# Probability buffers, the place of the late products and the bank of the second retention half in a two-layer decoder trunk

## The chip, the cores and the metric

The kernel runs on one core of one Trainium2 chip. The metric is the device time of one execution in microseconds, the median of several runs. TensorE multiplies matrices; ScalarE, VectorE and GpSimd work on elements; SyncE issues the transfers. In the rows these are PE (products) and PEld (weight loads), ACT, DVE, POOL and SP.

## The reference

Two layers, each on a residual stream of 256 tokens by 1024 channels. What matters here is the mixer, cut to its core:

```python
h = rmsnorm(x, norm_mix[i]); z = h @ w_in[i]           # q, k, v, gates, retention, merge columns
# attention, 2 groups of 4 heads, 2 blocks of 128 queries: three branches
p_cmp = masked_softmax(q @ k_cmp.T * scale, ...)       # 16 compressed keys
p_slc = masked_softmax(q @ k_s.T * scale, causal)      # all blocks are selected at this length
p_win = masked_softmax(q @ k_w.T * scale, causal)      # the window holds all 256 keys
y = g0 * (p_cmp @ v_cmp) + g1 * (p_slc @ v_s) + g2 * (p_win @ v_w)
# retention, 4 heads, chunks of 128
r = rms_noaffine((q_r @ k_r.T * decay) @ v_r) * silu(gate)
mix = sigmoid(merge_a) * (y @ w_up_nsa) + sigmoid(merge_b) * (r @ w_up_ret)
x = x + mix @ w_out
x = x + square(relu(rmsnorm(x) @ w_ff1)) @ w_ff2
x = x + sigmoid(rmsnorm(x) @ w_ple_gate) * (p @ w_ple)
```

## The kernel before

Everything is float32, and each matrix product with weights is three products of halves. A weight unit (128 x 1024) is loaded to a raw tile by SyncE and split into a high part (ScalarE copy, `hi`) and a low part (VectorE subtraction, `lo`), several units ahead of its use. A unit of 24 products of 256 columns is the usual grain. The units come in a fixed plan: first the columns of `w_in` (`kcvc`, `kvg`, `q`, `ksvs`, the compression weights `w`, retention `rq`, `rk`, `rv`, `rg`), then the merge columns `ma` and `mb` (8 units each), the up-projections `ua` and `ub` (4 each), `out`, and the MLP and the gated embedding.

The order on TensorE is that of the program text; the other engines' instructions are put in order by a scheduler from their dependences and priorities. While the kernel is built, a small planner keeps a virtual time for TensorE and for each other engine (`vt`, `charge`) and decides where the attention's and the retention's steps stand between the products of the weight units. These steps are generators in a background list. `poke`, called after each group of six products (three in the units of 512 columns), runs each generator whose due time is past; a generator yields its next due time, and `SLACK` adds to it by its name (1.0 for `attend`). The generators `attend` and `collect` also wait while ScalarE or VectorE is booked over 7 us ahead.

`attend` runs `softmax(g, t)` for the four turns (group, query block) and then the retention's `scores`. `softmax` issues per head the score products into two score banks of PSUM (`s_tile`), the masked maximum on VectorE and the exponentials on ScalarE into a probability tile `e`, and at the end the factor `cf` (gate over row sum). Its score products are due at the planned end of the bank's last reader (`sfin`) less `DE`. There are two probability buffers: one slot for the first query block (`S4` or `S2`), `S7` for the second, so the third and fourth softmax wait until the first and second turn are weighed. `collect` runs `weigh(g, t)` in the same order: GpSimd multiplies each block of `e` by its factor (3 blocks for the first query block, 5 for the second), TensorE transposes the block (`turn`), ScalarE and VectorE make high and low parts (`pp`, or `PC` for the 16 compressed keys), and two products add it to the accumulator bank `ot` (`apply`), of which there is one (`o_tile`). At the end `ot` is evacuated (`o`, two ScalarE and two VectorE instructions) and split to `NHh` and `NHl`, the input of `ua`. After the last turn `collect` runs `retain`: per query block the products of scores and values into `ot`, ScalarE's scaled copy, a norm with GpSimd's power, the gate, a transpose and a split, the input of `ub`.

The merge tensors `T` (tanh of `ma`, `mb`) lie in `S5` and `S6`; `S6` held `qn` before, `S7` held `ZB` before the probabilities and holds `MH` after them.

Of the kernel before, what the change touches and what calls it, by code (L numbers as in the profile page):

```python
# [15 lines left out]
P = 128  # L16
# [78 lines left out]
def trunk(ctx: ExitStack, tc: tile.TileContext, xT, wu, wg, cst, msk, par, pin, out):  # L95
# [34 lines left out]
    def o_tile(shape):  # L130
        return ps.tile(shape, F32, tag="ot", name=nm("ot"), bufs=1)
# [7 lines left out]
    def big(shape, tag, name, dt=F32):  # L139
        return bp.tile(shape, dt, tag=tag, name=nm(name))  # L140
# [39 lines left out]
    def fresh(t=None):  # L180
        cur[0] = vt["pe"] if t is None else t
# [191 lines left out]
    SL = 0.0  # L373
    DE = 0.5
    AHEAD_OF_SPLITS = ("compress",)
# [145 lines left out]
    def layer(l, st):  # L521
# [12 lines left out]
        qT = big([P, NH, S], "S3" if st["slot"] == 1 else "S1", "qT", F32R)  # L534
        e_tags = ["S4" if st["slot"] == 1 else "S2", "S7"]
        nc.gpsimd.memset(zs, 0.0)
# [120 lines left out]
        es, weighed, sfin, freed = {}, set(), [0.0, 0.0], [0.0]  # L657

        def softmax(g, t):
            e = big([P, HG, 272 if t == 0 else 528], e_tags[t], "e")  # L660
            nmx = small([P, HG, 3], "nmx")
# [32 lines left out]
            tt(out=cf, in0=cf, in1=gates[:, t, g * HG:(g + 1) * HG, :], op=ALU.mult)  # L694
            es[g, t] = e, cf

        def weigh(g, t):
            e, cf = es.pop((g, t))
            if t == 0:
                blocks = [(0, P, 0, V[:, 0, 0, g, :]), (144, P, 2, V[:, 1, 0, g, :]),  # L700
                          (128, 16, 1, VC[:, g, :])]
            else:
                blocks = [(0, P, 0, V[:, 0, 1, g, :]), (128, P, 0, V[:, 0, 0, g, :]),
                          (272, P, 2, V[:, 1, 0, g, :]), (400, P, 2, V[:, 1, 1, g, :]),
                          (256, 16, 1, VC[:, g, :])]
            n = len(blocks) - 1
            ot = o_tile([P, HG, P])
            parts = {}

            def scale(i):  # L710
                o, w, b, _ = blocks[i]
                gp(out=e[:, :, o:o + w], in0=e[:, :, o:o + w],
                   in1=cf[:, :, b:b + 1].to_broadcast([P, HG, w]), op=ALU.mult)

# [19 lines left out]

            fin, scaled = [], []
            t0 = cur[0]
            for i in range(n + 1):
                fresh(t0)
                scale(i)
                scaled.append(cur[0] + 3.0)  # L740
            yield scaled[0]
            turn(0)
            fin.append(cur[0])
            for i in range(1, n + 1):
# [5 lines left out]
                apply(i - 1)  # L750
            yield fin[n]
            apply(n)
# [18 lines left out]
        def attend():  # L771
            yield from until(lambda: NEED <= done)
            yield vt["pe"] + 1.5
            for i, x in enumerate(turns):
                if i > 1:
                    yield from until(lambda: turns[i - 2] in weighed)
                yield from softmax(*x)
            yield from until(lambda: (1, 0) in weighed)
            yield from scores()
            done.add("s")  # L780
# [27 lines left out]
        def scores():  # L808
            while not {("r", i, t) for i in range(2) for t in range(2)} <= done:
                yield vt["pe"] + 0.3  # L810
            d = big([P, 2, RH, 2, P], e_tags[0], "rs")
            sc_[0] = d
# [12 lines left out]
        def retain():  # L825
# [7 lines left out]
            for t in range(2):  # L833
                yield freed[-1]
                py = o_tile([P, RH, P])
                for h in range(RH):
# [158 lines left out]
        while not NEED <= done:  # L995
            pe_wait(vt["pe"] + 0.5)
            poke()
        T = [big([P, 8, S], f"S{5 + i}", "T") for i in range(2)]
        for i, name in enumerate(("ma", "mb")):
            for j in range(4):  # L1000
                pm = mm_tile([P, 2, S])
# [39 lines left out]
        drain()  # L1041
        MH = big([P, 8, S], "S7", "MH", F32R)
        ML = big([P, 8, S], "S8", "ML", F32R)
# [277 lines left out]
```

## Time and profile before

| | |
|---|---|
| time, median of 3 runs | 858.99 us (858.91 to 859.61) |
| the profiled execution | 859.11 us, its span 857.3 us |
| TensorE busy in the span | 842.5 us, 98% |
| VectorE, ScalarE, GpSimd busy | 602.6, 500.1, 78.6 us |
| TensorE clock granted, mean | 0.999 of 2.4 GHz |
| the weight load queue (q1) | 151.04 MB, 56.0% of 16 engines |

The page gives for each engine its busy time, and then the span in 40 slices with the busy share in tenths. A timeline row is: start in us, duration, engine, line, operation, what is written and read with shapes, the count of merged instructions, and in brackets the engine's idle time ahead of it and what ended that. The line named is mostly that of a helper (L220 products, L225 transposes, L188 ScalarE, L192, L200 and L208 VectorE, L214 GpSimd), so groups are told apart by their tiles. A wait row gives engine, line, releaser: us in total, times, the longest.

### The profile page before, as it was taken

How to read it: one execution, taken by the hardware profiler on the slowest of the kernel's cores; microseconds unless marked ns; L12 is line 12 of the kernel's file. 1: busy time of each engine (PE TensorE's matmuls, PEld its weight loads, DVE VectorE, ACT ScalarE, POOL GpSimd, SP SyncE). 2: the span in 40 equal slices, each digit the busy share in tenths (PEclk: the TensorE clock that was granted, in tenths of full speed). 3: DMA queues.
4: the chain of work that ended last, by engine and by line, in shares of the span. 5: the costliest groups of instructions: out<-in, count | busy, mean ns of one | idle time of the engine just before them, and what ended most of it. 6: DMA issues, size and time to landing. Idle time of an engine off the chain costs nothing.

```text
span 857.3 us, 16518 instructions
## 1 busy us (share of the span) xinstructions
PE 842.5 (98%) x6647; PEld 816.4 (95%) x6647; DVE 602.6 (70%) x977; ACT 500.1 (58%) x836; POOL 78.6 (9%) x68
## 2 busy tenths in 40 slices
PE   8999999999999999999999999999999999999997
PEld 7888899999999999999999988999999999999997
DVE  6897787686955555557789978776877555555584
ACT  6786876544744444445567768655456444445461
POOL 1240232010000000000004004121000000000000
PEclk9999999999999999999999999999999999999999
DMA  8877444356556665656555653643556656665641
GB/s 265 308 243 237 124 148 124 123 160 182 184 178 190 180 193 178 193 178 220 198 193 166 214 190 84 187 125 112 180 165 200 194 177 193 177 192 180 189 125 50
DMA packets 44284, 152.11 MB, mean 177 GB/s; under 512 B 5168, under 2 KB 6960, under 8 KB 44208
## 3 DMA queue, kind: packets, MB, share of 16 engines
q1 hardware_dynamic: 44064, 151.04, 56.0%
q8 instruction: 52, 0.85, 0.4%
q14 instruction: 24, 0.20, 0.1%
q10 hardware_dynamic: 144, 0.01, 0.0%
HBM read 149.99 MB, written 1.05 MB: 176 GB/s over the span
## 4 chain that ended last, share of the span: by engine, by line
PE 86%; DVE 6%; ACT 4%; DMA 1%; issue 1%; POOL 1%; SPq 0%; DVEq 0%; ACTq 0%; POOLq 0%
PE mm L220 49%; PE sc L220 17%; PE pt L220 14%; PE ot L220 4%; PE pt L225 2%; DVE lo L192 2%; ACT e L188 1%; ACT hi L188 1%; DMA raw<-in_wu_dram 1%; DVE e L208 1%; POOL e L214 0%; DVE o L192 0%; DVE zt L192 0%; ACT tmp L188 0%; ACT T L188 0%
## 5 line engine op out<-in xcount | busy, mean ns | idle before, releaser
L192 DVE TENSOR_TENSOR lo<-raw,hi 128x1024 fp32r<-128x1024 f32 (+2 forms) x287 | 345.3, 1210 | 186.7 <-ACT hi L188 185.5
L188 ACT ACTIVATE hi<-raw 128x1024 fp32r<-128x1024 f32 (+2 forms) x287 | 296.0, 1038 | 267.8 <-PE mm L220 155.6
L220 PE MATMUL mm<-XH,hi 128*128 128x256 f32 x992 | 283.6, 286 | 0.0
L220 PE MATMUL mm<-XH,lo 128*128 128x256 f32 x992 | 279.7, 282 | 0.0
L220 PE MATMUL mm<-XL,hi 128*128 128x256 f32 x992 | 279.4, 282 | 0.0
L220 PEld LDWEIGHTS mm<-XH,hi 128*128 128x128 f32 x992 | 187.0, 189 | 1.8
L220 PEld LDWEIGHTS mm<-XL,hi 128*128 128x128 f32 x992 | 187.0, 188 | 1.6
L220 PEld LDWEIGHTS mm<-XH,lo 128*128 128x128 f32 x992 | 186.9, 188 | 0.0
L220 PE MATMUL sc<-ho,hi 128*128 128x256 f32 x512 | 96.8, 282 | 0.0
L220 PE MATMUL pt<-ho,hi 128*128 128x256 f32 x512 | 96.6, 281 | 0.0
L220 PEld LDWEIGHTS sc<-ho,hi 128*128 128x128 f32 x512 | 78.6, 188 | 0.0
L220 PEld LDWEIGHTS pt<-ho,hi 128*128 128x128 f32 x512 | 78.6, 188 | 0.0
L220 PE MATMUL sc<-ho,lo 128*128 128x256 f32 x256 | 72.0, 281 | 0.0
L220 PE MATMUL pt<-ho,lo 128*128 128x256 f32 x256 | 72.0, 281 | 0.0
L220 PEld LDWEIGHTS pt<-ho,lo 128*128 128x128 f32 x256 | 48.2, 188 | 0.0
L220 PEld LDWEIGHTS sc<-ho,lo 128*128 128x128 f32 x256 | 48.2, 188 | 0.0
L214 POOL TENSOR_TENSOR e<-e,acf 128x512 f32<-128x512 f32 (+1 forms) x32 | 37.4, 1198 | 110.2 <-ACT hi L188 40.0
L220 PE MATMUL mm<-hi,XH 128*128 128x512 f32 (+2 forms) x128 | 44.4, 347 | 0.0
L220 PE MATMUL mm<-lo,XH 128*128 128x512 f32 (+2 forms) x128 | 43.7, 342 | 0.4 <-DVE lo L192 0.4
L220 PE MATMUL mm<-hi,XL 128*128 128x512 f32 (+2 forms) x128 | 43.7, 341 | 0.0
L188 ACT ACTIVATE e<-e,nmx 128x128 f32<-128x128 f32 (+2 forms) x96 | 37.6, 394 | 5.5 <-DVE nmx L208 5.2
L214 POOL TENSOR_TENSOR rso<-rsv,mhalf 128x2 f32<-128x2 f32 (+3 forms) x18 | 28.5, 1588 | 126.2 <-DVE rsv L196 126.2
(190 smaller groups left out, 1342.4 us busy)
## 6 DMA issues: line engine op xcount, KB each, us to landing
raw<-in_wu_dram SPq DMA_DIRECT2D x275, 512.0 KB, 3.7
raw<-in_wg_dram SPq DMA_DIRECT2D x8, 280.0 KB, 3.9
cst<-in_cst_dram SPq DMA_DIRECT2D x1, 768.0 KB, 6.3
out_dram<-XT SPq DMA_DIRECT2D x3, 256.0 KB, 2.4
XT<-in_xT_dram SPq DMA_DIRECT2D x4, 128.0 KB, 2.8
raw<-in_wu_dram SPq DMA_DIRECT2D x4, 128.0 KB, 3.3
XT<-in_xT_dram SPq DMA_DIRECT2D x2, 256.0 KB, 6.0
tmp<-in_pin_dram SPq DMA_DIRECT2D x2, 256.0 KB, 3.8
```

The lines of the kernel that those rows point to most:

```text
L188: return nc.scalar.activation(o, *a, **k)
L192: return nc.vector.tensor_tensor(**k)
L208: return nc.vector.tensor_tensor_reduce(**k)
L214: return nc.gpsimd.tensor_tensor(**k)
L220: return nc.tensor.matmul(o, a, b_, **k)
L225: return nc.tensor.transpose(o, a, i)
```

## The change

- There are three probability buffers: the first and third softmax use the slot they had, the second `S7`, the fourth `S6`. Only the third softmax still waits (for the first weighing).
- The factor's multiplications are issued at the end of `softmax`, right behind `cf`, instead of at the start of `weigh`; the planner puts the first transposes of a block at the planned end of its multiplication plus 1.6 instead of 3.0. The block of 16 compressed keys moves from the last place into the middle.
- The last product of a weighing is due `LATE` = 0.9 after the planned end of its low part, instead of at it; `DE` goes from 0.5 to 0.4.
- The second half of the retention's products goes into a score bank instead of the accumulator bank and is no longer held back by its planned release; the first half waits for the score banks' last planned reader too.
- `T` of `mb` moves to `S7` and is allocated when `mb` begins, and `MH` moves to `S6`.

```diff
@@ -371,7 +371,8 @@
     bg = []
     LB = 7.0
     SL = 0.0
-    DE = 0.5
+    DE = 0.4
+    LATE = 0.9
     AHEAD_OF_SPLITS = ("compress",)
     SLACK = {"kv_tail": 4.0, "q_tail": 3.0, "compress": 0.3, "attend": 1.0, "collect": 0.0}
 
@@ -532,7 +533,8 @@
         zs = big([P, 2, 16, 32], "B4", "zs")
         ZB = big([P, 16, 2, 2, 32], "S7", "ZB", F32R)
         qT = big([P, NH, S], "S3" if st["slot"] == 1 else "S1", "qT", F32R)
-        e_tags = ["S4" if st["slot"] == 1 else "S2", "S7"]
+        spare = "S4" if st["slot"] == 1 else "S2"
+        e_tags = {(0, 0): spare, (0, 1): "S7", (1, 0): spare, (1, 1): "S6"}
         nc.gpsimd.memset(zs, 0.0)
 
 
@@ -656,8 +658,16 @@
 
         es, weighed, sfin, freed = {}, set(), [0.0, 0.0], [0.0]
 
+        def branches(g, t):
+
+            if t == 0:
+                return [(0, P, 0, V[:, 0, 0, g, :]), (128, 16, 1, VC[:, g, :]),
+                        (144, P, 2, V[:, 1, 0, g, :])]
+            return [(0, P, 0, V[:, 0, 1, g, :]), (128, P, 0, V[:, 0, 0, g, :]), (256, 16, 1, VC[:, g, :]),
+                    (272, P, 2, V[:, 1, 0, g, :]), (400, P, 2, V[:, 1, 1, g, :])]
+
         def softmax(g, t):
-            e = big([P, HG, 272 if t == 0 else 528], e_tags[t], "e")
+            e = big([P, HG, 272 if t == 0 else 528], e_tags[g, t], "e")
             nmx = small([P, HG, 3], "nmx")
             sm = small([P, HG, 3], "smx")
             for h in range(HG):
@@ -692,25 +702,22 @@
             ts(out=cf, in0=sm, scalar1=1e-30, scalar2=None, op0=ALU.max)
             nc.vector.reciprocal(out=cf, in_=cf)
             tt(out=cf, in0=cf, in1=gates[:, t, g * HG:(g + 1) * HG, :], op=ALU.mult)
-            es[g, t] = e, cf
+            blocks = branches(g, t)
+            scaled = []
+            t0 = cur[0]
+            for o, w, b, _ in blocks:
+                fresh(t0)
+                gp(out=e[:, :, o:o + w], in0=e[:, :, o:o + w],
+                   in1=cf[:, :, b:b + 1].to_broadcast([P, HG, w]), op=ALU.mult)
+                scaled.append(cur[0] + 1.6)
+            es[g, t] = e, blocks, scaled
 
         def weigh(g, t):
-            e, cf = es.pop((g, t))
-            if t == 0:
-                blocks = [(0, P, 0, V[:, 0, 0, g, :]), (144, P, 2, V[:, 1, 0, g, :]),
-                          (128, 16, 1, VC[:, g, :])]
-            else:
-                blocks = [(0, P, 0, V[:, 0, 1, g, :]), (128, P, 0, V[:, 0, 0, g, :]),
-                          (272, P, 2, V[:, 1, 0, g, :]), (400, P, 2, V[:, 1, 1, g, :]),
-                          (256, 16, 1, VC[:, g, :])]
+            e, blocks, scaled = es.pop((g, t))
+
             n = len(blocks) - 1
             ot = o_tile([P, HG, P])
             parts = {}
-
-            def scale(i):
-                o, w, b, _ = blocks[i]
-                gp(out=e[:, :, o:o + w], in0=e[:, :, o:o + w],
-                   in1=cf[:, :, b:b + 1].to_broadcast([P, HG, w]), op=ALU.mult)
 
             def turn(i):
                 o, w, b, vv = blocks[i]
@@ -732,12 +739,7 @@
                 mm(ot, vv, ph.rearrange("p a b -> p (a b)"), start=i == 0, stop=False)
                 mm(ot, vv, pl.rearrange("p a b -> p (a b)"), start=False, stop=i == n)
 
-            fin, scaled = [], []
-            t0 = cur[0]
-            for i in range(n + 1):
-                fresh(t0)
-                scale(i)
-                scaled.append(cur[0] + 3.0)
+            fin = []
             yield scaled[0]
             turn(0)
             fin.append(cur[0])
@@ -748,7 +750,7 @@
                 fin.append(cur[0])
                 yield fin[i - 1]
                 apply(i - 1)
-            yield fin[n]
+            yield fin[n] + LATE
             apply(n)
             on = o2 = tmp([P, 2, P], tag="o", bufs=1)
             ov = ot.rearrange("p (c two) q -> p c two q", two=2)
@@ -772,7 +774,7 @@
             yield from until(lambda: NEED <= done)
             yield vt["pe"] + 1.5
             for i, x in enumerate(turns):
-                if i > 1:
+                if i == 2:
                     yield from until(lambda: turns[i - 2] in weighed)
                 yield from softmax(*x)
             yield from until(lambda: (1, 0) in weighed)
@@ -808,7 +810,7 @@
         def scores():
             while not {("r", i, t) for i in range(2) for t in range(2)} <= done:
                 yield vt["pe"] + 0.3
-            d = big([P, 2, RH, 2, P], e_tags[0], "rs")
+            d = big([P, 2, RH, 2, P], spare, "rs")
             sc_[0] = d
             for t in range(2):
                 for hp in range(2):
@@ -831,8 +833,9 @@
             ret["h"], ret["l"] = RHh, RHl
             yn, due_y = [None, None], [0.0, 0.0]
             for t in range(2):
-                yield freed[-1]
-                py = o_tile([P, RH, P])
+                if t == 0:
+                    yield max(freed[-1], sfin[-1])
+                py = (o_tile, s_tile)[t]([P, RH, P])
                 for h in range(RH):
                     vh = rV[:, :, h * P:(h + 1) * P]
                     for m in range(t + 1):
@@ -995,8 +998,9 @@
         while not NEED <= done:
             pe_wait(vt["pe"] + 0.5)
             poke()
-        T = [big([P, 8, S], f"S{5 + i}", "T") for i in range(2)]
+        T = {}
         for i, name in enumerate(("ma", "mb")):
+            T[i] = big([P, 8, S], ("S5", "S7")[i], "T")
             for j in range(4):
                 pm = mm_tile([P, 2, S])
                 for u in range(2):
@@ -1039,7 +1043,7 @@
             up(0, j)
             poke()
         drain()
-        MH = big([P, 8, S], "S7", "MH", F32R)
+        MH = big([P, 8, S], "S6", "MH", F32R)
         ML = big([P, 8, S], "S8", "ML", F32R)
         stf = new_stage(l, 1)
         for j in range(3):
```

## Rows read from the trace of the kernel before

**Rows 1.** The page: its first line, TensorE's busy time, and the granted TensorE clock in 40 slices.

```profile
span 857.3 us, 16518 instructions
...
PE 842.5 (98%) x6647; PEld 816.4 (95%) x6647; DVE 602.6 (70%) x977; ACT 500.1 (58%) x836; POOL 78.6 (9%) x68
...
PEclk9999999999999999999999999999999999999999
```

**Rows 2.** Busy time by stretch: the attention and retention stage of the first and of the second layer. Columns: start and end, length, then busy us and count for PE, PEld, DVE, ACT and POOL, the granted clock, the DMA share and GB/s.

```profile
84.00:184.00 100.00, 97.63 (x737) 92.33 (x736) 77.44 (x192) 68.74 (x169) 21.64 (x18) 1.00 0.43 132
...
505.00:606.00 101.00, 98.26 (x741) 92.88 (x740) 77.91 (x192) 69.15 (x169) 21.63 (x18) 1.00 0.44 133
```

**Rows 3.** All waits of TensorE's products from 84 to 184 us, the first layer's stage.

```profile
PE ot L220 <- ACT tmp L188: 0.9, 1, 0.9
PE ot L220 <- DVE PC L192: 0.7, 1, 0.7
PE pt L225 <- POOL e L214: 0.6, 1, 0.6
PE sc L220 <- DVE nmx L208: 0.2, 1, 0.2
```

**Rows 4.** The same from 505 to 606 us, the second layer's stage; the two rows left out read as the first and the third of rows 3.

```profile
...
PE ot L220 <- DVE PC L192: 0.8, 1, 0.8
...
PE sc L220 <- DVE nmx L208: 0.5, 1, 0.5
```

**Rows 5.** Timeline of TensorE around the first transposes of probabilities.

```profile
94.21 0.40 PE L220 MATMUL mm<-hi,XL 128*128 128x512 f32 x1
95.23 0.66 PE L225 MATMUL pt<-cst,e 128*128 128x128 f32 x4 [0.62 <-POOL e L214]
```

**Rows 6.** Of the chain of waits there: GpSimd's first multiplication (start, us).

```profile
93.25 1.94 POOL e L214
```

**Rows 7.** Timelines of TensorE and of VectorE around the last products of the third weighing.

```profile
143.74 0.39 PE L220 MATMUL ot<-PC,VC 128*128 128x512 f32 x1
144.87 0.50 PE L220 MATMUL ot<-PC,VC 128*128 128x512 f32 x1 [0.74 <-DVE PC L192]
...
143.00 1.22 DVE L192 TENSOR_TENSOR lo<-raw,hi 128x1024 fp32r<-128x1024 f32 x1
144.14 0.67 DVE L192 TENSOR_TENSOR PC<-pt,PC 16x512 fp32r<-16x512 f32 x1
```

**Rows 8.** Timelines of TensorE and of ScalarE around the two halves of the retention.

```profile
169.63 0.28 PE L220 MATMUL mm<-NHh,lo 128*128 128x256 f32 x1
170.76 0.49 PE L220 MATMUL ot<-rV,rs 128*128 128x128 f32 x2 [0.85 <-ACT tmp L188]
...
170.03 0.67 ACT L188 ACTIVATE tmp<-ot,r 128x512 f32<-128x512 f32 x1
```

**Rows 9.** Timelines of TensorE and of VectorE around a score product of the third softmax.

```profile
108.88 0.28 PE L220 MATMUL mm<-XL,hi 128*128 128x256 f32 x1
109.00 0.28 PE L220 MATMUL mm<-XH,lo 128*128 128x256 f32 x1
109.44 0.49 PE L220 MATMUL sc<-KT,qT 128*128 128x272 f32 x2 [0.16 <-DVE nmx L208]
...
107.11 0.72 DVE L200 SCALAR_TENSOR_TENSOR rG<-tmp,rG 128x512 f32<-128x512 f32 x1
```

**Rows 10.** Busy time in stretches of 6 us from 104 to 164 us: two of the ten, and the sum of all ten. Columns as in rows 2.

```profile
104.00:110.00 6.00, 5.84 (x49) 5.67 (x48) 5.08 (x23) 5.94 (x19) 3.76 (x4) 1.00 0.00 0
110.00:116.00 6.00, 6.00 (x53) 6.00 (x52) 6.00 (x11) 5.84 (x19) 2.17 (x2) 1.00 0.43 101
...
sum 60.00, PE 59.10 PEld 57.46 DVE 46.44 ACT 40.79 POOL 14.55; mean PE 5.91 PEld 5.75 DVE 4.64 ACT 4.08 POOL 1.46
```

**Rows 11.** Timelines of GpSimd (its multiplications for the third and the fourth turn) and of TensorE (the first transposes of these turns).

```profile
120.75 2.31 POOL L214 TENSOR_TENSOR e<-e,acf 128x512 f32<-128x512 f32 x3 [8.57 <-DVE acf L192]
143.08 6.30 POOL L214 TENSOR_TENSOR e<-e,acf 128x512 f32<-128x512 f32 x5 [20.02 <-ACT hi L188]
...
136.71 0.60 PE L225 MATMUL pt<-cst,e 128*128 128x128 f32 x4
...
154.32 0.60 PE L225 MATMUL pt<-cst,e 128*128 128x128 f32 x4
```

**Rows 12.** Timelines of TensorE and of VectorE at the end of the first and of the second weighing: the last products into the accumulator bank, and the last part of its evacuation.

```profile
103.18 0.62 PE L220 MATMUL ot<-PC,VC 128*128 128x512 f32 x2
...
106.22 0.86 DVE L192 TENSOR_TENSOR o<-ot,o 64x256 f32<-64x256 f32 x2 [0.15 <-PE sc L220]
...
126.91 0.62 PE L220 MATMUL ot<-PC,VC 128*128 128x512 f32 x2
...
128.59 0.86 DVE L192 TENSOR_TENSOR o<-ot,o 64x256 f32<-64x256 f32 x2 [0.35 <-ACT o L188]
```

**Rows 13.** Timeline of TensorE: the products of two neighbouring blocks of the fourth weighing.

```profile
157.32 0.62 PE L220 MATMUL ot<-pp,V 128*128 128x512 f32 x2
...
159.66 0.63 PE L220 MATMUL ot<-pp,V 128*128 128x512 f32 x2
```

**Rows 14.** Timeline of VectorE: two weight splits that follow each other, the second beside a multiplication on GpSimd.

```profile
98.94 1.23 DVE L192 TENSOR_TENSOR lo<-raw,hi 128x1024 fp32r<-128x1024 f32 x1
...
109.91 2.10 DVE L192 TENSOR_TENSOR lo<-raw,hi 128x1024 fp32r<-128x1024 f32 x1
```

## The prediction

> **What bounds the kernel now.** I read the page's head first: TensorE is busy in 842.5 of 857.3 us, at its upper clock level (2.4 GHz) throughout [rows 1]. So time can only come out of the 14.8 us in which TensorE stands idle, or be lost by making it stand idle more; work saved on another engine counts for nothing by itself. Second, the busy time by stage: the edits touch the attention and retention stage of each layer, 84 to 184 us and 505 to 606 us, where TensorE is idle for 2.37 and 2.74 us [rows 2]. Third, what TensorE waited for inside these stages: four waits in each layer, the same four in both [rows 3, 4]. That short list is the whole ground for a gain.
>
> The view's idle times are a little short, since the ends of pipelined products are modelled; the start of one product after the start of the one ahead tells it better. The transposes of the first probability block start at 95.23, after a product that started at 94.21 and would have let the next one go 0.23 us later (two such products take 0.62, one 0.39): 0.79 us lost for the 0.62 shown [rows 5, 7, 12]. In the same way: 0.32 us at the score products of 109.44 (products of 256 columns start 0.12 apart) [rows 9]; 144.87 less 143.74 less 0.23 = 0.90 at the last product of an attention block [rows 7]; 170.76 less 169.63 less 0.12 = 1.01 at the second retention half [rows 8]. Sum 3.02 us in the first layer. In the second, with the same 0.16 added to each wait: 0.79 + 0.67 + 0.91 + 1.01 = 3.38. Together **6.4 us is all that there is to win**.
>
> **The change part by part.**
>
> *Second retention half in a score bank.* The wait at 170.76 ended when ScalarE's copy of the first half out of the accumulator bank ended, at 170.03 + 0.67 = 170.70 [rows 8]. In a score bank the second half's products need nothing of that copy; the score banks were last read for the retention scores, which stand ahead of the last weighing in the order. Gain 1.0 us a layer, the surest term. What is late next: the second half's own copy, with weight products to cover it.
>
> *Late products (LATE, 0.9).* At 144.87 the low half of an attention block's last product waited for VectorE's subtraction, 0.67 us at 144.14, which stood behind a weight split of 1.22 us that started at 143.00 [rows 7]. The planner believed VectorE free there. Before, the last product followed at the planned end of the subtraction; now 0.9 us later. Background work looks at the clock only between groups of six products, 0.71 us at 0.12 each [rows 9], so the product moves one or two groups, 0.7 to 1.4 us, past this 0.90. Nothing is added, since weight products fill the place. Behind the product stands the evacuation of the accumulator, which has cover (below). Gain 0.7 to 0.9; I take 0.9. At the other three block ends TensorE did not wait, so the edit costs and gives nothing there.
>
> *Scaling in the softmax, due 1.6 instead of 3.0 after it.* GpSimd runs the same 16 multiplications a layer; none is added, and no DMA moves with them. GpSimd already starts a set when its factor is there, whenever the weighing stands in the text (the third set was released by its factor) [rows 11], and only a few reciprocal roots share its queue, so the moved emission is worth nothing on that engine. What moves is the planner's belief. For the first set it had counted from the score products: 1.88 for the multiplication and 3.0 of margin, 4.88. Now it counts from the factor: some 2.1 for maxima, exponentials and factor, then 1.88 and 1.6, in all 5.6. The first transposes are so placed 0.7 us later or more, one group of three wide products, and the 0.79 at 95.23, which ended when GpSimd's first multiplication did at 95.19 [rows 6], shrinks to about 0.1. Gain 0.7. For later sets it goes the other way: the set that began at 120.75 was transposed only at 136.71, the one of 143.08 at 154.32 [rows 11], since the planner let the scaling begin with the weighing. These waits cost TensorE nothing: weight products ran there. Gone, they only move attention work forward.
>
> *Three probability buffers, the others re-placed.* The fourth softmax no longer waits for the second weighing. By itself this too is worth zero: products covered that wait. The attention can end up to 17 us sooner: 128.1 instead of 136.7 for the third weighing's first transposes, and 145.9 instead of 154.3 for the fourth's [rows 7, 11, 12]. The new neighbours cost nothing: the merge tensor in the second buffer is first written after the eight units of the first merge weights, long after that buffer's last transposes; the third buffer's next writer comes after the up-projection, which began near 169 [rows 8].
>
> *DE, 0.5 to 0.4.* Score products ask for their bank 0.1 us later. Of the wait at 109.44, where VectorE was held by a 0.72 us gate product [rows 9], 0.1 goes or, with the groups' grid, all or nothing: 0 to 0.32 and 0 to 0.67. I take 0.1 in each layer, the plain shift.
>
> *What comes new.* Weighings now follow each other at once, and all use one accumulator bank. Its evacuation ends 106.22 + 0.86 = 107.08, 3.3 us after the first weighing's last products end (103.80), and 1.9 us after those of the second (127.53 to 129.45) [rows 12]. The next weighing needs the bank about 3.0 us after those products: from block to block they stand 2.34 apart with two groups between [rows 13], and at a hand-over a third group comes to it, 0.71. So the wait is 0 with the short lag, 0.3 with the long one. Two hand-overs a layer become tight. I take 0.3 for each, the long lag being the row with most other work around it: 1.2 us in all; the ends are 0 and, with a second split in front, 1.5 each, 6.0.
>
> Sum: 2 x (1.0 + 0.9 + 0.7 + 0.1) = 5.4 gained, 1.2 lost, 4.2 net. The profiled execution took 859.11 us, 1.8 more than its span, and stands 0.1 above the median of 858.99. I take 4.2 from the median: **854.8 us**.
>
> **The rivals.**
>
> *A. The stalls move.* The gain is eaten by waits at the accumulator hand-overs and the score banks. At 1.5 us for each of four hand-overs the net is 0.6 lost: 859.6; at half that, 856.6. For it: the attention really becomes denser, and ScalarE was busy in 5.94 and 5.84 of 6 us where it was densest [rows 10]. Against: in that densest stretch TensorE lost only 0.16 of idle time in 12 us.
>
> *B. VectorE comes late, slower than before.* The fourth softmax now falls beside the second and third weighing, eight blocks a layer. Each block's subtraction can end up behind a weight split, as once it did, at 0.9 us [rows 7]. Six such stalls in the whole kernel undo the 5.4; eight give 860.8, all sixteen 868.0. What would push it there: a split beside GpSimd's scaling took 2.10 us at 109.91, against 1.23 at 98.94 [rows 14]. The Trainium skill (GPSIMD Engine Reference, § 8 Key points) says that GpSimd shares its SBUF interfaces with VectorE and contends with VectorE instructions that have two SBUF inputs, as a split has; the trace agrees in this pair of rows, and the rule speaks against moving scaling into a fuller stretch. Against B: VectorE was busy 46.44 us of the 60 between 104 and 164 [rows 10]. Take out 17 us, with six weight units of 24 products (2.9 us each) and so six splits of 1.22 and three products of 0.7, and 37 of 43 us are left, 86%; between 110 and 116 it was busy 6.00 of 6 while TensorE lost nothing. And the splits have reserve: none started between 98.94 and 109.91, 11 us, and no product waited for a split in either stage [rows 3, 14].
>
> *C. It does not do what it says.* The groups' grid can put the late products and the first transposes where they were, or the bank change meets another wait: then only part of the 5.4 comes, 0 to 2: 857 to 859.
>
> **How the numbers follow.** My forecast's own case (net 1.8 to 6.4) has 0.66; A 0.17, mostly near zero; B 0.12; C 0.05. A measurement of this kernel can tell about 0.2%, 1.7 us, from no change. So faster by more: 0.68 (the forecast's case and a little of A and C); within: 0.20; slower by more: 0.12, all of B. The lower end is all waits gone and no new one, 852.6, with 0.2 for the run's own spread: 852.4. The upper end leaves out B and the worse half of A and C: 858.4.
>
> **What would show it.** Right: no wait of TensorE on ScalarE's copy at the retention's second half; none at the last product of the third weighing; the first transposes without a wait on GpSimd; the third weighing's transposes right behind the second's last product; TensorE idle in each stage at about 0.5 to 1 us instead of 2.4 and 2.7. Wrong: idle time of TensorE at the accumulator right after a weighing (A), several waits on VectorE's subtractions between 110 and 150 us (B), or the four waits still in their places (C). A change outside the two stages would be of a kind that I have not counted at all.

## The result and the profile after

The changed kernel takes 853.84 us (median of 4 runs, 853.19 to 854.43), the kernel before in the same job 858.95 us (858.74 to 859.61). The ratio is 0.9938, 95% interval 0.9926 to 0.9951: faster by 5.1 us. The profiled execution took 853.69 us, 1.8 more than its span.

The page of the changed kernel, its first line and TensorE's; answers to [rows 1]:

```profile
span 851.9 us, 16528 instructions
...
PE 840.6 (99%) x6647; PEld 816.6 (96%) x6647; DVE 605.1 (71%) x977; ACT 499.8 (59%) x836; POOL 77.5 (9%) x68
```

The span is 5.4 us shorter. TensorE's idle time fell from 14.8 to 11.3 us. The other 1.9 us came out of its busy time, from which the prediction's opening says no time can come (its counts from start to start take in a part of it): a product that waits is booked longer (0.50 instead of 0.39 in [rows 7]).

Busy time of the changed kernel in the two stages, columns and stretches as in [rows 2], and all waits of its products from 84 to 192 us, which answer to [rows 3]:

```profile
84.00:184.00 100.00, 99.29 (x758) 94.68 (x757) 80.92 (x194) 69.45 (x170) 20.65 (x18) 1.00 0.44 137
505.00:606.00 101.00, 100.29 (x775) 96.10 (x774) 82.14 (x196) 69.97 (x170) 20.65 (x18) 1.00 0.45 139
```

```profile
PE mm L220 <- DVE RHl L192: 0.7, 1, 0.7
```

All four waits of each layer are gone, and one new one stands in their place, for `RHl`, the low part of the retention's output and so of the input of `ub`. The same single wait is in the second layer. It is the whole of TensorE's 0.71 us of idle time in each stage.

The old places in the changed kernel, from TensorE's timelines; they answer to [rows 5], [rows 12], [rows 7, 11] and [rows 8]. The fourth old wait, at the third softmax's score products [rows 9], is missing from the row of waits above:

```profile
96.52 0.65 PE L220 MATMUL sc<-KT,qT 128*128 128x272 f32 x4
97.01 0.60 PE L225 MATMUL pt<-cst,e 128*128 128x128 f32 x4
...
108.07 0.63 PE L220 MATMUL ot<-pp,V 128*128 128x512 f32 x2
...
124.32 0.65 PE L220 MATMUL sc<-KT,qT 128*128 128x272 f32 x4
...
132.35 0.63 PE L220 MATMUL ot<-pp,V 128*128 128x512 f32 x2
...
133.53 0.60 PE L225 MATMUL pt<-cst,e 128*128 128x128 f32 x4
...
146.06 0.62 PE L220 MATMUL ot<-pp,V 128*128 128x512 f32 x2
...
164.59 0.62 PE L220 MATMUL ot<-pp,V 128*128 128x512 f32 x2
...
165.75 0.28 PE L220 MATMUL mm<-NHh,hi 128*128 128x256 f32 x1
...
167.18 1.05 PE L220 MATMUL ot<-rV,rs 128*128 128x128 f32 x8
168.07 1.06 PE L220 MATMUL sc<-rV,rs 128*128 128x128 f32 x8
```

No row has a bracket. The two last products of a weighing run as a pair (x2), those of the third too (146.06), where the old wait stood; the first transposes (97.01) wait for nothing, the third weighing's transposes (133.53) stand one group behind the second's last product, the fourth softmax starts at 124.32, ahead of the end of the second weighing, and the two halves of the retention follow each other. But the last weighing ends at 164.59 + 0.23, only 0.9 us sooner than before, and the units of `ua` begin 0.9 us behind that (165.75); before, they began 3.2 us behind it.

The new wait, in the timelines of TensorE, of VectorE and of GpSimd in the changed kernel:

```profile
180.74 0.28 PE L220 MATMUL mm<-RHh,hi 128*128 128x256 f32 x1
181.73 0.39 PE L220 MATMUL mm<-RHl,hi 128*128 128x256 f32 x1 [0.71 <-DVE RHl L192]
...
176.47 1.14 DVE L200 SCALAR_TENSOR_TENSOR tmp<-tmp,rso,rG 128x128 f32<-128x128 f32 x4 [0.53 <-POOL rso L214]
...
178.13 1.21 DVE L192 TENSOR_TENSOR lo<-raw,hi 128x1024 fp32r<-128x1024 f32 x1
179.26 0.68 DVE L200 SCALAR_TENSOR_TENSOR T<-T,mm 128x512 f32<-128x512 f32 x1
179.86 1.22 DVE L192 TENSOR_TENSOR lo<-raw,hi 128x1024 fp32r<-128x1024 f32 x1
180.99 0.68 DVE L192 TENSOR_TENSOR RHl<-pt,RHh 128x512 fp32r<-128x512 f32 x1
...
175.43 1.01 POOL L214 TENSOR_TENSOR rso<-rsv,mhalf 128x4 f32<-128x4 f32 x1 [3.79 <-DVE rsv L196]
```

The product at 181.73 would have started 0.12 after the one at 180.74, so 0.87 us are lost there, 0.97 with the slower start of the products that follow. Of the kernel before, the same two places:

```profile
184.19 0.28 PE L220 MATMUL mm<-RHh,hi 128*128 128x256 f32 x1
184.31 0.28 PE L220 MATMUL mm<-RHl,hi 128*128 128x256 f32 x1
...
183.46 0.69 DVE L192 TENSOR_TENSOR RHl<-pt,RHh 128x512 fp32r<-128x512 f32 x1
```

There `RHl` was ready at 184.15, 0.16 us ahead of its first use. From the first product of the retention to the first of `ub` TensorE had 16.05 us of other work before (168.14 to 184.19) and has 13.56 now (167.18 to 180.74); the chain to the end of `RHl` took 16.0 us and takes 14.5. It became shorter, but its cover shrank more.

So the account, from the first product of `ub` in each layer (184.19 to 180.74; 605.95 to 599.53, of which 2.48 came from layer one): 3.45 and 3.94 gained, 0.97 lost twice, 5.4 in all.

### The profile page after: what moved, and what is told of

Same layout as the page of the kernel before. It is cut to its first block, busy times and chain, and to the rows that moved or that the text cites. A ratio compares the mean times of both kernels' runs of the same rounds, so it can differ in the third digit from the quotient of the medians.

```text
span 851.9 us, 16528 instructions
## 1 busy us (share of the span) xinstructions
PE 840.6 (99%) x6647; PEld 816.6 (96%) x6647; DVE 605.1 (71%) x977; ACT 499.8 (59%) x836; POOL 77.5 (9%) x68
## 4 chain that ended last, share of the span: by engine, by line
PE 89%; DVE 6%; DMA 1%; ACT 1%; issue 1%; POOL 1%; SPq 0%; DVEq 0%; ACTq 0%
PE mm L220 51%; PE sc L220 18%; PE pt L220 14%; PE ot L220 4%; PE pt L225 2%; DVE lo L192 2%; DMA raw<-in_wu_dram 1%; POOL rso L214 1%; DVE tmp L200 0%; ACT hi L188 0%; DVE zt L192 0%; ACT tmp L188 0%; DVE yss L204 0%; DVE T L200 0%; DVE zs L192 0%
## 5 line engine op out<-in xcount | busy, mean ns | idle before, releaser
L214 POOL TENSOR_TENSOR r<-ms,mhalf 128x2 f32<-128x2 f32 x6 | 6.6, 1100 | 365.2 <-DVE ms L196 337.0
```

The lines of the kernel that those rows point to most:

```text
L214: return nc.gpsimd.tensor_tensor(**k)
```

## The experiments

The expectations number the theories. Theory 1 is the prediction's: each part takes away its own wait, and the gains add. Theory 2 is the rival that each of the first four expectations names, and not the same in all: a wait removed alone comes back elsewhere (the bank and `LATE`), or the part at hand brings most of the gain (the scaling and the third buffer). Theory 3 was made after the first four runs, theory 4 as its rival for the run with `LATE` off and two buffers, theory 5 after theory 3 fell. All ratios are to the kernel before in the same job (858.9 to 859.6 us); lengths of spans are those of the profiled executions.

**One part alone, on the kernel before.** The score bank:

```diff
-                yield freed[-1]
-                py = o_tile([P, RH, P])
+                if t == 0:
+                    yield max(freed[-1], sfin[-1])
+                py = (o_tile, s_tile)[t]([P, RH, P])
```

> The kernel before with the second retention half in a score bank and nothing else. Theory 1 (each part is worth the wait that it removes at its own place): the wait of TensorE on ScalarE's copy at the retention's second half (0.9 us in the view, 1.0 from start to start) is gone in both layers, the three other waits stay; 2.0 us less. Theory 2 (the parts pay only together, by a denser attention, and a wait removed alone comes back at the next place): the first product of the up-projection of the retention waits instead, and the time is within 0.5 us of before.

Measured: 856.71 us, 0.9971 (0.9960 to 0.9983), span 854.9. The wait on ScalarE's copy is gone, the other three of [rows 3] are in their places. The 2.4 us are 1.2 a layer, near the term of 1.0: theory 1.

`LATE` alone:

```diff
+    LATE = 0.9
...
-            yield fin[n]
+            yield fin[n] + LATE
```

> The kernel before with the last product of each weighing 0.9 us later in the plan and nothing else. Theory 1: the wait on the compressed block's low part at the end of the third weighing (0.7 and 0.8 us in the view, 0.9 from start to start) is gone in both layers, the others stay; 1.8 us less, 1.4 if the group grid leaves a part. Theory 2: the weighings end later, the softmax that waits for them too, and the wait turns up at the score products; within 0.5 us of before.

Measured: 867.80 us, 1.0101 (1.0088 to 1.0115), span 866.1. No theory had this. The wait at the third weighing's last product is gone, as theory 1 said, but others came. Waits of TensorE's products in this kernel, 84 to 192 us, and from its timeline the second weighing's last products, the fourth softmax's first, and the end of the attention:

```profile
PE sc L220 <- DVE rs L192: 1.0, 1, 1.0
PE ot L220 <- DVE pp L192: 0.9, 1, 0.9
PE mm L220 <- DVE RHl L192: 0.8, 1, 0.8
PE mm L220 <- ACT NHh L188: 0.8, 1, 0.8
...
```

```profile
130.92 0.62 PE L220 MATMUL ot<-PC,VC 128*128 128x512 f32 x2
...
132.80 0.53 PE L220 MATMUL sc<-KT,qT 128*128 128x272 f32 x3
...
170.24 0.49 PE L220 MATMUL ot<-PC,VC 128*128 128x512 f32 x1 [0.21 <-DVE PC L192]
170.57 0.28 PE L220 MATMUL mm<-NHh,hi 128*128 128x256 f32 x1
```

The second weighing ends 4.0 us later than in [rows 12], the fourth softmax, which waits for its buffer, starts 4.0 later (128.82 before), and the attention ends 4.5 later. By then all products of the merge columns are used up: `ua` follows the attention's last product at once, and every step of the chain stands bare.

The scaling in the softmax alone (two buffers, `DE` 0.5, the block of 16 keys in the middle):

```diff
+            blocks = branches(g, t)
...
+                gp(out=e[:, :, o:o + w], in0=e[:, :, o:o + w],
+                   in1=cf[:, :, b:b + 1].to_broadcast([P, HG, w]), op=ALU.mult)
+                scaled.append(cur[0] + 1.6)
```

> The kernel before with the scaling at the end of the softmax, due 1.6 us after it, the block of compressed keys in the middle, and two probability buffers as before; no later last product, no score bank. Theory 1: the wait of the first transposes on GpSimd (0.6 us in the view, 0.8 from start to start) is gone in both layers; the wait at the retention's second half stays; 1.4 to 1.6 us less, and the third and fourth weighing start right behind the one ahead. Theory 2: this is the part that makes the attention dense, so it brings most of the 5.1 us by itself, 3 us or more.

Measured: 854.73 us, 0.9949 (0.9935 to 0.9962), span 852.9. Its waits from 84 to 192 us:

```profile
PE ot L220 <- ACT tmp L188: 0.6, 1, 0.6
PE ot L220 <- DVE pp L192: 0.3, 1, 0.3
```

Three of the four waits of [rows 3] are gone by this part alone, and a smaller one (0.3) is new at the second weighing's last product; the span is 4.4 us shorter: theory 2, and three times the term of 0.7 a layer. The part holds two edits, the early scaling and the block of 16 keys in the middle, and no run takes them apart.

The third buffer alone (with the new places of `T` and `MH`):

```diff
...
+        e_tags = {(0, 0): spare, (0, 1): "S7", (1, 0): spare, (1, 1): "S6"}
...
-                if i > 1:
+                if i == 2:
```

> The kernel before with the third probability buffer and the two tensors that change places for it, and nothing else: the fourth softmax doesn't wait for the second weighing. Theory 1: products covered that wait, so the four waits stay about where they are; within 0.6 us of before. Theory 2: it is the heart of the change; 2 us less or more.

Measured: 862.86 us, 1.0051 (1.0038 to 1.0063), span 861.0. Neither theory. The fourth softmax starts at 119.58, but the weighings beside it end later (147.21 for the third against 144.87, 167.35 for the last against 165.74), and `ua` at 167.59 has no merge products left ahead of it:

```profile
170.80 0.38 PE L220 MATMUL mm<-NHh,hi 128*128 128x256 f32 x1 [1.60 <-ACT NHh L188]
```

Added up, the four parts alone make the span longer by 5.7 us (-2.4, +8.8, -4.4, +3.7); together, with `DE`, they make it 5.4 shorter. Theory 1 is dead: the parts do not add. **Theory 3**: what counts is the margin between the attention's last product and the first of `ua`. Where it is gone, each step costs its own length. `LATE` uses it up; the third buffer pays for that.

**One part taken out of the change.** Two buffers:

```diff
-        e_tags = {(0, 0): spare, (0, 1): "S7", (1, 0): spare, (1, 1): "S6"}
+        e_tags = ["S4" if st["slot"] == 1 else "S2", "S7"]
...
-                if i == 2:
+                if i > 1:
```

> The changed kernel with two probability buffers (the fourth softmax waits for the second weighing again, T and MH at their old places). Theory 3 (formed after the first runs: merge-weight products are the only cover for the attention, and what counts is whether its last product comes before they run out; in the changed kernel that margin is 0.9 us): the second weighing ended at 132.6 us, the fourth softmax began at 124, so it would start some 8 us later; the attention ends after the merge products, with waits in the last weighing and at the first up-projection as in b_late; 4 us slower than the changed kernel or more. Theory 1: the buffer is worth nothing, within 0.6 us of the changed kernel.

Measured: 863.98 us, 1.0057 (1.0044 to 1.0071), span 862.2, 10.3 longer than with three. Theory 3 had the direction.

`LATE` off:

```diff
-    LATE = 0.9
+    LATE = 0.0
```

> The changed kernel with LATE = 0. Theory 3: each weighing ends about a microsecond earlier, the margin ahead of the up-projection grows by 2 us or more; one or two waits at the end of a weighing come back, as the 0.5 us in b_scale; 0.5 to 1.5 us slower than the changed kernel in all. Theory 1: the two waits of 0.9 us come back, 1.8 us slower. Should the wait at the low part of RHl (0.97 from start to start) go with the earlier end, the two nearly cancel.

Measured: 853.22 us, 0.9932 (0.9920 to 0.9945), span 851.5. Theory 1 had 1.8 us more and missed. Theory 3 had 0.5 to 1.5 more, or next to nothing should the wait for `RHl` go; that wait went, but none of the four old ones came back. The margin grew to 6.5 us (last product 162.06, `ua` 168.52), and the wait for `RHl` gave way to one of 0.2 us at the transposes of the retention, on VectorE's gate product (`tmp`).

The difference from the whole change, 0.4 us of span, is not to be told from none. With three buffers, `LATE` is not needed.

The bank undone (the diff of the first run, turned round):

> The changed kernel with the second retention half in the accumulator bank again, behind its planned release. Theories 1 and 3 alike: the wait on ScalarE's copy comes back with 0.7 to 1.0 us in each layer, and the retention ends later, so the wait at the low part of RHl stays or grows by the same; 1.4 to 4 us slower than the changed kernel.

Measured: 854.53 us, 0.9945 (0.9933 to 0.9957), span 852.7: 0.8 worse than the change in span, not clear of the noise, and less than the 2.4 that the bank gave alone. Both theories had 1.4 or more and missed: the copy's wait did not come back, and the wait for `RHl` fell to 0.4.

The pause of the second half dropped:

```diff
-                    if t == 1 and h == 1:
-                        yield vt["pe"]
```

> The changed kernel without the pause of one product group in the middle of the second retention half (two lines of retain left out). If the new wait at the first product of the retention's up-projection is one of order (VectorE has a weight split and a merge product ahead of the last low part RHl, and the chain of the second half is one group late), both low parts now come ahead of that split in VectorE's order, the wait of 0.7 us (0.97 from start to start) goes in both layers, 1.9 us less than the changed kernel. If the chain is late by its own length, the wait stays within 0.3 us of what it was.

Measured: 855.87 us, 0.9963 (0.9951 to 0.9976), span 854.5; 1.08 of the 2.6 more lay ahead of the stage. The wait for `RHl` went, another of the same kind came:

```profile
PE pt L225 <- DVE tmp L200: 1.1, 1, 1.1
```

So that wait is not one instruction's: in the change and in these two variants of it the retention's chain is about as long as its cover, and one of its steps is late. Here some 0.9 of the 1.1 us goes back to GpSimd's power, which took 1.91 us instead of 1.01 (last section). With a larger margin the wait is small or gone: 0.2 us with `LATE` off (margin 6.5), none in the run below with the scaling and the bank alone (4.2).

**Theory 3 tried.** `LATE` off and two buffers (both diffs above), and `LATE` doubled to 1.8:

> The changed kernel with LATE = 0 and two probability buffers (the merge tensors in their old places); scaling in the softmax and the score bank stay. It closes a square of four: both on 853.8, LATE off 853.2, third buffer off 864.0, now both off. Theory 3 (what counts is the margin between the attention's last product and the end of the merge products; the third buffer is needed only because LATE uses the margin up): the last product stays about 3 us ahead of the first ua product, as in the early-scaling kernel (span 852.9), and the score bank takes its copy wait of 0.6 a layer away: 852.5 to 854, within 1 us of the changed kernel. Theory 4 (the third buffer is worth its 10 us in itself, whatever LATE is): 862 to 864.

> The changed kernel with LATE = 1.8 instead of 0.9. Theory 3: each of the four last products moves one group or so further, the attention's end moves by 1 to 3 us, the margin of 0.9 us is gone, and the products of the last weighing or of the retention wait for other engines with no merge product left between: 856 to 862, with waits of TensorE between 160 and 185 us. Rival (a late product only changes places with weight products, and the margin plays no part): 853.3 to 854.4, within 0.5 us of the changed kernel.

Measured: 864.07 us, 1.0050 (1.0037 to 1.0064), span 863.0, and 854.24 us, 0.9940 (0.9928 to 0.9952), span 853.0. Theory 3 missed both. Without `LATE`, going back to two buffers loses as much as with it, and with three buffers a double `LATE` costs 0.4 us, not to be told from none, with the margin unchanged at 0.9 (165.09 to 166.03). What `LATE` does depends on the buffers, and something else than `LATE` makes two buffers slow here.

Against the early-scaling kernel, which has two buffers as well and took 854.7, only the bank and `DE` differ. TensorE's instructions first part in order at the score products of the first two softmaxes, from 88 us on: a group more of three wide products comes ahead of them, long before the bank is used. Hence **theory 5**: `DE`. The last run is the kernel before with the scaling and the bank alone; against the run with two buffers and `LATE` off it has one number changed:

```diff
-    DE = 0.4
+    DE = 0.5
```

> The kernel before plus two parts alone: the scaling in the softmax and the score bank. It differs from the kernel with LATE off and two buffers (864.1) in one number, DE = 0.5 instead of 0.4, and from the early-scaling kernel (854.7) in the score bank alone. Theory 5 (DE = 0.4 is what the third buffer has to pay for: it moves score products of the first softmaxes by a group, the first weighing ends 3.7 us later, at 108.06 instead of 104.40, and with two buffers the third softmax waits for just that): the first weighing ends near 104.4, and the time is that of the early-scaling kernel less its one wait on ScalarE's copy, 0.6 to 0.7 us a layer: 852.8 to 854.2, no worse than the whole change. Theory 4 (two buffers cost the 10 us themselves once the retention's half is in a score bank): 862 to 865.

Measured: 853.05 us (852.77 to 854.42), 0.9928 (0.9914 to 0.9942), span 852.6. Theory 5, to the microsecond, and theory 4 (two buffers cost the 10 us themselves) is out. The place where the two kernels part, the first softmax's third head, first with `DE` 0.5 and then with 0.4:

```profile
89.01 0.41 PE L220 MATMUL sc<-KT,qT 128*128 128x272 f32 x2
...
89.04 0.41 PE L220 MATMUL sc<-KT,qT 128*128 128x272 f32 x2
```

The softmax's first products stand at 87.10 and 86.44, so these come 1.91 and 2.60 us behind them, after six wide products and after nine. TensorE's timeline in the slow one of the pair (`DE` 0.4): last products of the first and second weighing, first score products of the fourth softmax, end of the attention and `ua`:

```profile
107.83 0.63 PE L220 MATMUL ot<-pp,V 128*128 128x512 f32 x2
...
130.41 0.63 PE L220 MATMUL ot<-pp,V 128*128 128x512 f32 x2
...
133.89 0.53 PE L220 MATMUL sc<-KT,qT 128*128 128x272 f32 x3
...
168.69 0.50 PE L220 MATMUL ot<-pp,V 128*128 128x512 f32 x1 [0.96 <-DVE pp L192]
169.03 0.28 PE L220 MATMUL mm<-NHh,hi 128*128 128x256 f32 x1
...
171.39 0.38 PE L220 MATMUL mm<-NHh,hi 128*128 128x256 f32 x1 [0.77 <-ACT NHh L188]
```

The same in the fast one (`DE` 0.5), whose only wait from 84 to 192 us is the one in the second row:

```profile
104.86 0.62 PE L220 MATMUL ot<-pp,V 128*128 128x512 f32 x2
...
128.24 0.50 PE L220 MATMUL ot<-pp,V 128*128 128x512 f32 x1 [0.35 <-DVE pp L192]
...
131.59 0.53 PE L220 MATMUL sc<-KT,qT 128*128 128x272 f32 x3
...
164.89 0.63 PE L220 MATMUL ot<-pp,V 128*128 128x512 f32 x2
...
169.27 0.37 PE L220 MATMUL mm<-NHh,hi 128*128 128x256 f32 x1
```

A first weighing that ends 3.0 us later makes the second end 2.4 later, the fourth softmax start 2.3 later and the attention end 3.6 later. The 4.2 us between its end and `ua` become 0.3, and TensorE stands bare at its last products, at `NHh` and at `RHl`. The whole stage began 0.7 us earlier in the slow run (86.44 against 87.10), so counted from there each of these delays is 0.7 longer. The table puts the runs side by side (us, starts of TensorE's products in the first layer; the first score products start at 85.9 to 86.4 in all of them but the third, which has 87.10):

| kernel | buffers | 2nd weighing's last | 4th softmax's first | attention's last | `ua` | time |
|---|---|---|---|---|---|---|
| before | 2 | 127.14 | 128.82 | 165.74 | 168.95 | 859.0 |
| scaling | 2 | 127.56 | 130.91 | 164.44 | 167.70 | 854.7 |
| scaling, bank | 2 | 128.24 | 131.59 | 165.12 | 169.27 | 853.1 |
| the same, `DE` 0.4 | 2 | 130.64 | 133.89 | 168.69 | 169.03 | 864.1 |
| the same, `DE` 0.4, `LATE` 0.9 | 2 | 131.33 | 134.57 | 168.55 | 168.89 | 864.0 |
| `LATE` alone | 2 | 131.15 | 132.80 | 170.24 | 170.57 | 867.8 |
| third buffer alone | 3 | 128.01 | 119.58 | 167.35 | 167.59 | 862.9 |
| the change | 3 | 132.59 | 124.32 | 164.82 | 165.75 | 853.8 |
| the change, `LATE` 1.8 | 3 | 132.85 | 124.16 | 165.09 | 166.03 | 854.2 |
| the change, `LATE` 0 | 3 | 131.96 | 123.97 | 162.06 | 168.52 | 853.2 |

With two buffers the fourth softmax starts 1.6 to 3.4 us after the second weighing, and whatever delays that weighing goes through to the end; with three it starts some 8 us before it, and the delay stays where it is. Of the margin theory one half holds: the four kernels slower than before are the four whose margin (from the attention's last product to `ua`) is down to 0.2 or 0.3 us. Above that the time does not follow it: 0.9 and 6.5 us of margin go with 853.8 and 853.2.

**A try at the last wait.** The steps of the retention's norm ahead of the weight splits by priority, `LATE` off:

```diff
+                with tc.high_priority():
                     y = tmp([P, RH, P])
...
```

> The changed kernel with LATE = 0 and the steps between the retention's products and its transposes (scaled copy, squares, sums, root, gate product) put ahead of the weight splits on ScalarE and VectorE by priority. Theory: the wait that is left with LATE = 0, 0.41 us a layer at the retention's transposes on VectorE's gate product, goes; nothing of the same size takes its place, since weight splits have reserve: 852.0 to 852.8. Rival (the chain is only as late as its own length, VectorE's queue plays no part, or the pushed splits make the weight products wait): 853.0 to 855.

Measured: 853.28 us, 0.9925 (0.9913 to 0.9938), span 851.5, with the same wait of 0.2. The order of VectorE's and ScalarE's instructions came out the same as without it, so the run does not test the theory. The run shows how well a time repeats: 853.22 and 853.28.

## Why the prediction was right, and where its steps were not

The time lay 1.0 us from the forecast and the mechanism in the large was right: TensorE bounds, its four waits a layer in the two stages were the ground for a gain, and all four went. Two parts suffice for that: the scaling takes three of them and the bank the fourth. The terms behind the sum were mostly of other sizes, and two of them were not gains at all.

*The score bank, 1.0 a layer*: 1.2 alone. Right. Inside the whole change it is worth no more than 0.8 in the two layers together, since the retention's chain is the next thing late; "the second half's own copy, with weight products to cover it" looked one step down that chain and not to its end.

*Scaling, 0.7 a layer*: 2.2 alone. Mis-sized. The step counted the first transposes' wait. The part also took the waits at the third weighing's last product and at the score products, which the prediction gave to `LATE` and `DE`. In this part the block of 16 keys is no longer last, so that its subtraction, `PC`, is not what a weighing ends on. How much of the 2.2 is the block's new place and how much the scaling, no run shows.

*`LATE`, 0.9 a layer*: this step failed. "Nothing is added, since weight products fill the place" holds at the product itself. But a weighing's end also lets the next softmax into its buffer. Alone it costs 8.8 us; in the change it gives nothing: with it off, the wait at this product does not come back.

*The third buffer, "by itself this too is worth zero"*: it failed both ways, 3.7 us lost alone and 10.3 kept in the change. The waiting it removes costs nothing where there is margin, and that was all the rows of before could show. What it does in the change is to cut the path by which later weighings delay the end: with `DE` 0.4 and `LATE` off, three buffers take 853.2 us and two 864.1. Why it loses when alone is open: its weighings come later, and no run took that apart.

*`DE`, 0.1 a layer*: this step failed too. The prediction named the grid of groups but priced the move by the wait at one product. With two buffers it costs 10 to 11 us (864.07 against 853.05, spans 863.0 and 852.6), because it puts a group more ahead of the first softmaxes' score products. `DE` 0.5 with three buffers was not run.

*"The attention can end up to 17 us sooner"*: 0.9. The transposes of the last weighing came at 152.56, 1.8 sooner, not 8.4. The third softmax starts 4.2 later than before (109.96 against 105.77), behind a first weighing that ends 4.9 later (108.30), and the fourth, begun at 124.32, has its factor only at 144.75 + 0.17, so that GpSimd begins its multiplications 2.0 us later than before ([rows 11], 143.08), though that softmax began 4.5 us sooner:

```profile
144.75 0.17 DVE L192 TENSOR_TENSOR acf<-acf,gates 128x12 f32<-128x12 f32 x1
145.16 2.03 DVE L192 TENSOR_TENSOR lo<-raw,hi 128x1024 fp32r<-128x1024 f32 x1 [0.24 <-ACT hi L188]
...
145.07 5.49 POOL L214 TENSOR_TENSOR e<-e,acf 128x512 f32<-128x512 f32 x5 [19.95 <-DVE acf L192]
```

*Accumulator hand-overs, 1.2 lost*: 0 (rival A at the accumulator did not happen). What was lost instead is the wait for `RHl`, 1.9 us in both layers, in no part of the sum. So the net of 4.2 came out as 7.4 gained less 1.9. That is 1.0 more than the 6.4 us that were "all that there is to win"; some 0.7 of it is in the rows: the product behind a waiting one starts later too, which the prediction's count leaves out. In the kernel before, the waiting group at 170.76 [rows 8] gave way to the next product after 0.91 us, the same group without a wait (172.47) after 0.81; at the three other waits the difference is 0.06 to 0.11. The other 0.3 is not settled.

*Rival B, VectorE late*: no product of a block waited for a subtraction. Windows of 6 us of the changed kernel from 104 to 164 us, the sum, which answers to [rows 10]:

```profile
sum 60.00, PE 60.00 PEld 58.61 DVE 49.81 ACT 41.33 POOL 14.37; mean PE 6.00 PEld 5.86 DVE 4.98 ACT 4.13 POOL 1.44
```

VectorE did get fuller, by 3.4 us, and TensorE was never idle in those 60. The contention was there (the split at 145.16 took 2.03 us beside GpSimd's multiplication, as in [rows 14]), and the splits' reserve bore it.

The prediction was right in its sum partly by luck: too little from the scaling, too much from `LATE` and a loss at the wrong place.

## What to carry to other kernels

A wait that costs nothing where it stands may still hold a chain that runs out of cover 40 us later: for each step that is put off, ask who is let in by its end, and follow that to the place where the covering work ends. The margin there (the last product of the chain against the first product that needs it) says more than the list of waits, since it shows what comes next when it is gone. When several edits come together, try them alone and left out: here two of the five gave the whole gain, and the third buffer paid for what `DE` had cost. That it pays for `LATE` as well is not shown: `LATE` cost 8.8 us in the kernel before, and no run adds the third buffer alone to it.

## What the hardware showed that was not expected

GpSimd's power of 128 x 4 elements, in the retention's norm, has two durations, and what VectorE had just begun decides. Timelines of GpSimd and of VectorE in the kernel without the pause:

```profile
171.71 1.01 POOL L214 TENSOR_TENSOR rso<-rsv,mhalf 128x4 f32<-128x4 f32 x1 [20.07 <-DVE rsv L196]
175.24 1.91 POOL L214 TENSOR_TENSOR rso<-rsv,mhalf 128x4 f32<-128x4 f32 x1 [2.52 <-DVE rsv L196]
...
175.07 1.22 DVE L192 TENSOR_TENSOR lo<-raw,hi 128x1024 fp32r<-128x1024 f32 x1
177.19 1.14 DVE L200 SCALAR_TENSOR_TENSOR tmp<-tmp,rso,rG 128x128 f32<-128x128 f32 x4 [0.90 <-POOL rso L214]
```

The power that began 0.17 us after a weight split (175.07) took 1.91 us, the split its usual 1.22. In the changed kernel the power at 175.43 ran beside a product of `T` with a PSUM tile (VectorE, 175.26) and took 1.01. In the kernel before (176.39) and in the one with the bank undone (171.31 and 175.96) the powers began 0.17 to 0.18 us after the start of a split and took 1.91 each. In all fourteen kernels every retention power that began so took 1.91 us, and every other one 1.01. The Trainium skill (GPSIMD Engine Reference, § 8 Key points) says that GpSimd contends with VectorE instructions that have two SBUF inputs; the rows agree. Here it is GpSimd that pays; in [rows 14] and at 145.16, where the multiplication began first (109.89 and 145.07), it is the split. In each of these pairs of a split and a GpSimd instruction the one that began second took longer. Since VectorE then waits for the root (0.90 us above), a split issued just ahead of the power lengthens the chain that ended up late.
